# Every TensorE instruction of a hybrid decoder step kept in the order in which the program emits it

## The chip, the cores and the metric

The kernel runs on one core of one Trainium2 chip, in one launch. The time is device microseconds of that core. The core's engines take instructions each from a queue of its own, in that queue's order, and wait for each other on semaphores: TensorE (PE; its weight loads are shown apart as PEld), VectorE (DVE), ScalarE (ACT), GpSimd (POOL) and SyncE (SP), which here issues all the DMA transfers.

## The reference, cut to what matters

One layer of a hybrid decoder, for a prompt of 2048 tokens and for 8 sequences of 8 sample tokens, in float32. Three head groups share one RMSNorm, one input projection and one output projection:

```python
u = rmsnorm(h, norm_w)
proj = u @ w_in                      # 1024 -> z, xbc, dt, gq, gk, gv, gg, glr, sq, sk, sv, sg
y_ssd = ...   # causal conv, silu, chunked state-space scan, gated group norm
y_gla = ...   # decayed linear attention in chunks of 64, per-head norm, silu gate
y_swa = ...   # RMS norm of q and k, window-128 attention with bias and sinks, silu gate
mix = concat([y_ssd, y_gla, y_swa]) @ w_out
h = h + mix
h = h + sigmoid(h @ w_pg) * (p @ w_pe)
```

It returns the two outputs and the new states and caches.

## The kernel before, in words

The tokens are cut into 8 blocks of 256 (17 tiles of 128, the last of them the 64 sample tokens, which ride with block 1). A product in float32 accuracy is made of three products of rounded parts (high by high, high by low, low by high), so a projection unit is 24 matmuls into one PSUM tile: `dense_F` (features on the partitions, 256 columns, or 320 in block 1), `dense_T` (tokens on the partitions, 280 or 512 columns). `mm` (L204) and `tr` (L207) are the helpers that issue nearly every matmul and transpose, the latter also on TensorE.

The kernel goes through the blocks in stages. In G it normalizes and transposes x (`prep_chain`: x tile in X7 or X8, transposes `pt`, then `uh` and `ul` by ACT L326 and DVE L327), projects q, k (`pq`, `pk_`), v and gates (`pT`) and runs the linear attention (`gla_a`: `ptl`, `py`; `gla_b`: `pk`, `pa`, `pu`, `po`, `pn`, for the sample tokens also `pos` and `pU`). In W it projects q, k, v of the window attention (`pT`, 512 columns, `u_qkv`), norms them (ACT L688, DVE L690, POOL L691 and L693, DVE L696 and L698), transposes them (`pq`, `swa_turn`), splits them (ACT L729, DVE L730), makes logits `pl`, the softmax (DVE L768, ACT L743), its transposes `ptp` and the output `po`; between them stand the gate units `pg`. S is the convolution and scan (`pfx`, `pfz`, `pbt`, `pcb`, `pxt`, `pys`, `pst`), O the output projection and the last stage the per-layer gate, both by a Strassen-like scheme of seven products (class `Square`, `product`, 12 matmuls of 512 columns each: `pX`, `pY`, `pZ`, `pV`).

Two things set the order of the work. The first is the kernel's own planner, class `Order`: it emits large dense units one after another (each with a cost in us, such as 2.62 for 24 matmuls of 256 columns) and, in between, steps of chains (generators such as `gla_a` or `swa_tile`) as soon as they are due on its running sum of costs. How long a chain's next step is held back is a number in the table `LAT`:

```python
LAT = {
    "x_s": 0.0, "x_t": 2.2, "u": 2.6, "T": 0.3, "glT": 0.0, "A": 10.2, "As": 10.9, "kT": 3.0, ...
    "sqg": 3.3, "ve": 0.8, "qk": 0.5, "kF": 1.4, "qF": 1.7, "sm": 10.8, ...
```

`"qk"` is the time from the end of a `u_qkv` unit to the step that transposes its tile, `"glT"` that from `ptl` to `py`. The second is the scheduler of the tile framework: it is given the instructions as emitted, and for each engine makes a queue by its own estimate of when each is ready, so that a matmul emitted later may stand ahead of one emitted earlier. That queue is then fixed; the chip does not reorder it. Pools (`psM` three PSUM buffers, `psF` and `psT` two each, `psU` one) make an instruction wait until the buffer it takes is free; the transposes `pt` of blocks 1 to 7 and `pq` of W use `psU`.

Of the kernel before, what the change touches and what calls it, by code (L numbers as in the profile page):

```python
# [149 lines left out]
def hybrid_step(ctx: ExitStack, tc: tile.TileContext, I, C, O):  # L150
    nc = tc.nc
    od = Order()
    PE, V, A, G, SP = nc.tensor, nc.vector, nc.scalar, nc.gpsimd, nc.sync
# [47 lines left out]
        SP.dma_start(out=t, in_=src)  # L201
        return t

    def mm(out, lhsT, rhs, start=True, stop=True):  # L204
        PE.matmul(out, lhsT=lhsT, rhs=rhs, start=start, stop=stop)  # L205

    def tr(out, in_, idn):  # L207
        PE.transpose(out, in_, idn)  # L208


    uh_d = [tc.dram_tile([128, 8, ncols(b)], F32, name=f"uhd{b}") for b in range(NB)]
# [54 lines left out]
    def dense(ps, pairs):  # L266
        n = len(pairs)
        for i, (lh, ll, rh, rl) in enumerate(pairs):
            mm(ps, lh, rh, i == 0, False)
            mm(ps, lh, rl, False, False)  # L270
            mm(ps, ll, rh, False, i == n - 1)
# [36 lines left out]
    def prep_chain():  # L308
        for b in range(NB):
            if b >= 2:  # L310
                yield 0, 0, ("U", b - 2)
            n = ncols(b)
            uh = up.tile([128, 8, n], F32R, tag="uh", name="uh")
            ul = up.tile([128, 8, n], F32R, tag="ul", name="ul")
            for i, (tt, c0, rows) in enumerate(tiles_of(b)):
                if i == 2:
                    load_x(b, i)
                xt = loaded.pop((b, i))
                for q in range(2):
                    yield 0.45, LAT["x_s"] if i == 2 and q == 0 else LAT["x_t"]  # L320
                    pt = mps([128, 4, 128], "pt") if b == 0 else psU.tile([128, 4, 128], F32, tag="u", name="pt")
                    for j in range(4):
                        k = 4 * q + j
                        tr(pt[:, j, :rows], xt[:rows, 128 * k:128 * k + 128], ident[:rows, :rows])
                    o = uh[:, 4 * q:4 * q + 4, c0:c0 + rows]
                    A.activation(out=o, in_=pt[:, :, :rows], func=AF.Copy)  # L326
                    V.tensor_tensor(out=ul[:, 4 * q:4 * q + 4, c0:c0 + rows], in0=pt[:, :, :rows],  # L327
                                    in1=o.bitcast(F32), op=ALU.subtract)
                if b == 0 and i == 0:
                    od.mark("u0", LAT["u"])  # L330
                    us["G", 0] = uh, ul
            us["G", b] = uh, ul
            od.mark(("u", "G", b), LAT["u"])
            SP.dma_start(out=uh_d[b], in_=uh.bitcast(F32))
            SP.dma_start(out=ul_d[b], in_=ul.bitcast(F32))
            for i in range(2):
                if b + 1 < NB:
                    load_x(b + 1, i)
# [137 lines left out]
    def gla_a(b):  # L476
# [5 lines left out]
        for (tt, c0, rows), g in zip(tl, gl):  # L482
            tr(ptl[:, c0:c0 + rows], g[:rows, 0:16], ident[:rows, :rows])
# [38 lines left out]
    def gla_b(b):  # L522
# [6 lines left out]
        for i, (tt, c0, rows) in enumerate(tl):  # L529
            tr(pk[:rows, i, :], kd[:, c0:c0 + rows], ident)  # L530
# [843 lines left out]
    def rows(i):  # L1374
        return 64 if i == NT else 128
# [117 lines left out]
    class Square:  # L1493
# [36 lines left out]
        def product(self, g, n):  # L1530
            R = rows(self.groups[g][0])
            p, akey, bkey = self.prods(g)[n]
            first = p in ("P1", "P6", "P7", "P5") or (self.sample(g) and p == "P3")
            if first:
                self.ps[g, BANK[p]] = self.bank(g, BANK[p])
            ps, a, b = self.ps[g, BANK[p]], self.op[g, akey], ws[self.w, bkey]
            for k in range(4):
                for i, (x, y) in enumerate(((0, 0), (0, 4), (1, 0))):
                    PE.matmul(ps[:R], lhsT=a[:, x, k, :R], rhs=b[:, y + k], start=first and k + i == 0, stop=k == 3 and i == 2,  # L1539
                              skip_group_check=True)  # L1540
            if p == "P6":

                self.u2 = (dk if self.w == "g" else ck).tile([128, 512], F32, tag="u2", name="u2")
                A.activation(out=self.u2[:R], in_=self.ps[g, "X"][:R], func=AF.Copy)
                V.tensor_tensor(out=self.u2[:R], in0=self.u2[:R], in1=ps[:R], op=ALU.subtract if self.sample(g) else ALU.add)
# [329 lines left out]
```

## Time and profile before

| | |
|---|---|
| median of 3 runs | 1224.53 us (1223.22 to 1225.87) |
| the profiled execution: its own time | 1223.86 us |
| its span, first to last instruction | 1222.0 us |
| PE busy | 1168.4 us, 96% |
| PEld busy | 983.9 us, 81% |
| DVE, ACT, POOL busy | 59%, 40%, 36% |
| mean granted TensorE clock | 0.987 |

The span lies 1.9 us below the time of the same execution. A matmul is shown from its start to a modelled end, and the next one starts before that end; the time that a run of matmuls takes is read from one start to the next. "Busy" is the union of these intervals, so the span less PE's busy time, 53.6 us, is the time in which no matmul was in flight. In a timeline row, the text in brackets at the end is the idle time of the engine before it and what ended that. Names are those of the program's tiles without their numbers, so a box that holds many tiles has one name: `X_G` is the x tile (and small vectors) in stage G, `Y_G`, `w_G`, `X_W` other boxes.

### The profile page before, as it was taken

Reading aid. Unit: us, or ns where it says so; the run is one execution under the profiler, and the core shown is the slowest. Engines: PE = TensorE matmul, PEld = TensorE weight load, DVE = VectorE, ACT = ScalarE, POOL = GpSimd, SP = SyncE. Lnnn points to the kernel's source line nnn. Section 1 sums busy time; section 2 is a strip of 40 time slices with the busy share of each in tenths; the row PEclk is TensorE's granted clock in tenths of the full one; section 3 lists DMA queues with packets and bytes.
Section 4 is the critical chain, followed back from the end, with each engine's and each line's share of the span. In section 5 each row is a group of like instructions: output and inputs, shape, how many; then the busy total and the mean of one; then the engine's idle time right before and its main releaser. Section 6 shows DMA issues by size and latency. Waiting matters only on the chain. (4 is left out here: it accounts for less than half of the span.)

```text
span 1222.0 us, 20943 instructions
## 1 busy us (share of the span) xinstructions
PE 1168.4 (96%) x8010; PEld 983.9 (81%) x8010; DVE 720.3 (59%) x1476; ACT 484.4 (40%) x994; POOL 441.8 (36%) x505
## 2 busy tenths in 40 slices
PE   7899999998999999899999999899899999999997
PEld 7787887687888889798799898777778877788886
DVE  4766565744544356478767668877666683444552
ACT  4443434551444445444345435563122352233331
POOL 4222224224521112626534433445445322233431
PEclk8899999999999999899999999999999999999999
DMA  8745465276642237503413333567676432222221
GB/s 249 225 178 194 160 240 165 71 222 178 199 138 100 99 131 229 197 26 129 154 60 121 129 139 97 172 210 238 230 263 212 144 112 87 88 78 78 95 78 52
DMA packets 119036, 182.33 MB, mean 149 GB/s; under 512 B 35573, under 2 KB 88293, under 8 KB 112792
## 3 DMA queue, kind: packets, MB, share of 16 engines
q1 hardware_dynamic: 118936, 180.99, 45.0%
q8 instruction: 63, 1.03, 0.4%
q14 instruction: 37, 0.30, 0.1%
HBM read 125.59 MB, written 55.37 MB: 148 GB/s over the span
## 5 line engine op out<-in xcount | busy, mean ns | idle before, releaser
L205 PE MATMUL pfx<-uh,w 128*128 128x256 f32 (+1 forms) x768 | 151.5, 292 | 3.7 <-ACT Y_S L1094 3.0
L205 PEld LDWEIGHTS pfx<-uh,w 128*128 128x128 f32 x768 | 122.3, 191 | 8.4 <-ACT Y_S L1094 3.7
L205 PE MATMUL pfx<-ul,w 128*128 128x256 f32 (+1 forms) x384 | 110.3, 287 | 0.0
L205 PE MATMUL pfz<-uh,w 128*128 128x256 f32 (+1 forms) x512 | 102.8, 293 | 3.9 <-DVE Y_S L1121 2.5
L205 PE MATMUL pg<-uh,w 128*128 128x256 f32 (+1 forms) x512 | 102.8, 293 | 1.6 <-DVE Y_W L891 1.6
L1690 POOL TENSOR_TENSOR X_C<-ul_D,X_C 128x512 f32<-128x512 f32 (+1 forms) x33 | 43.0, 1303 | 135.7 <-DVE ul_D L1689 111.9
L205 PEld LDWEIGHTS pfz<-uh,w 128*128 128x128 f32 x512 | 82.3, 191 | 7.0 <-DVE Y_S L1121 3.3
L205 PE MATMUL pT<-w,uh 128*128 128x512 f32 (+1 forms) x272 | 87.9, 400 | 0.0
L205 PEld LDWEIGHTS pg<-uh,w 128*128 128x128 f32 x512 | 82.7, 192 | 4.4 <-DVE Y_W L891 1.8
L205 PE MATMUL pg<-ul,w 128*128 128x256 f32 (+1 forms) x256 | 74.6, 292 | 0.0
L205 PEld LDWEIGHTS pfx<-ul,w 128*128 128x128 f32 x384 | 73.2, 191 | 1.5 <-issue 1.3
L205 PE MATMUL pfz<-ul,w 128*128 128x256 f32 (+1 forms) x256 | 74.0, 289 | 0.0
L205 PE MATMUL pT<-Y_G,uh 128*128 128x280 f32 (+1 forms) x272 | 63.5, 317 | 2.7 <-ACT uh L326 2.5
L229 DVE TENSOR_TENSOR w<-raw,w 128x1024 fp32r<-128x1024 f32 x32 | 44.4, 1401 | 29.4 <-ACT w L227 29.4
L227 ACT ACTIVATE w<-raw 128x1024 fp32r<-128x1024 f32 x40 | 41.6, 1056 | 47.2 <-DMA raw<-in_w_in_dram 20.9
L205 PEld LDWEIGHTS pT<-w,uh 128*128 128x128 f32 (+1 forms) x272 | 48.8, 185 | 12.1 <-issue 1.8
L1689 DVE SCALAR_TENSOR_TENSOR ul_D<-ul_D,peC 128x512 f32<-128x512 f32 (+1 forms) x34 | 23.3, 685 | 53.7 <-PE peC L205 48.1
L1539 PE MATMUL pZo<-w,X_C 128*128 128x512 f32 x192 | 48.3, 403 | 6.2 <-DVE X_C L1595 6.2
L205 PE MATMUL pT<-w,ul 128*128 128x512 f32 (+1 forms) x136 | 53.9, 397 | 0.0
L205 PE MATMUL peC<-Y_P,uh_C 128*128 128x512 f32 (+1 forms) x204 | 52.8, 393 | 0.8 <-DVE ul_D L1689 0.8
L205 PEld LDWEIGHTS pT<-Y_G,uh 128*128 128x128 f32 (+1 forms) x272 | 46.2, 197 | 7.5 <-ACT uh L326 3.6
L205 PEld LDWEIGHTS pg<-ul,w 128*128 128x128 f32 x256 | 49.3, 193 | 0.9 <-issue 0.4
(442 smaller groups left out, 2983.2 us busy)
## 6 DMA issues: line engine op xcount, KB each, us to landing
uh<-uhd SPq DMA_DIRECT2D x14, 1024.0 KB
ul<-uld SPq DMA_DIRECT2D x14, 1024.0 KB
raw<-in_w_in_dram SPq DMA_DIRECT2D x17, 512.0 KB
X_G<-in_x_prompt_dram SPq DMA_DIRECT2D x16, 512.0 KB
Y_S<-afd SPq DMA_DIRECT2D x16, 512.0 KB
X_C<-in_x_prompt_dram SPq DMA_DIRECT2D x16, 512.0 KB
ul_C<-mixd SPq DMA_DIRECT2D x16, 512.0 KB
out_y_prompt_dram<-X_C SPq DMA_DIRECT2D x16, 512.0 KB
```

Of the source, the lines that this page charges most:

```text
L205: PE.matmul(out, lhsT=lhsT, rhs=rhs, start=start, stop=stop)
L227: A.activation(out=hi[:, k0:k1], in_=rw, func=AF.Copy, scale=scale)
L229: eng.tensor_tensor(out=lo[:, k0:k1], in0=rw, in1=hi[:, k0:k1].bitcast(F32), op=ALU.subtract)
L1539: PE.matmul(ps[:R], lhsT=a[:, x, k, :R], rhs=b[:, y + k], start=first and k + i == 0, stop=k == 3 and i == 2, skip_group_check=True)
L1689: V.scalar_tensor_tensor(out=th, in0=th, scalar=1.0, in1=pe[:R], op0=ALU.add, op1=ALU.mult)
L1690: eng.tensor_tensor(out=h[:R, cs], in0=th, in1=h[:R, cs], op=ALU.add)
```

## The change

`mm` and `tr` hand each instruction to `tc.keep_in_program_order`, and the products of class `Square` go through `mm` as well, so all matmuls and transposes are covered. The queue of TensorE is then the order of emission, that is the planner's. Other engines' instructions are still placed by the scheduler.

```diff
-    def mm(out, lhsT, rhs, start=True, stop=True):
-        PE.matmul(out, lhsT=lhsT, rhs=rhs, start=start, stop=stop)
+    def mm(out, lhsT, rhs, start=True, stop=True, **kw):
+        tc.keep_in_program_order(PE.matmul(out, lhsT=lhsT, rhs=rhs, start=start, stop=stop, **kw))
 
     def tr(out, in_, idn):
-        PE.transpose(out, in_, idn)
+        tc.keep_in_program_order(PE.transpose(out, in_, idn))
@@
-                    PE.matmul(ps[:R], lhsT=a[:, x, k, :R], rhs=b[:, y + k], start=first and k + i == 0, stop=k == 3 and i == 2,
-                              skip_group_check=True)
+                    mm(ps[:R], a[:, x, k, :R], b[:, y + k], first and k + i == 0, k == 3 and i == 2, skip_group_check=True)
```

The number of instructions on TensorE stays the same. Counted over both queues, the runs of matmuls that follow each other into one PSUM tile go from 1274 to 987.

At the start, TensorE's queue before (`pt_257` and `pt_292` transpose the second x tile, in X8, `pT_264` projects the first tile, `pT_320` the second):

```order
L208 MATMUL pt_243<-ident_127,X7_G_139 128x128 x4
L208 MATMUL pt_250<-ident_127,X7_G_139 128x128 x4
L205 MATMUL pT_264<-Y0_G_147,uh_241 128x280 x2
...
L205 MATMUL pT_264<-Y0_G_147,uh_241 128x280
L208 MATMUL pt_257<-ident_127,X8_G_156 128x128 x4
L208 MATMUL pt_292<-ident_127,X8_G_156 128x128 x4
L205 MATMUL pT_320<-Y0_G_147,uh_241 128x280 x2
L205 MATMUL pq_355<-uh_241,w256_171 128x256
L205 MATMUL pk__388<-uh_241,w256_171 128x256
```

The same stretch after the change (`pt_313` and `pt_348` transpose the third x tile, which is loaded into X7 when the first has been used):

```order
L208 MATMUL pt_250<-ident_127,X7_G_139 128x128 x4
L208 MATMUL pt_257<-ident_127,X8_G_156 128x128 x4
L205 MATMUL pT_264<-Y0_G_147,uh_241 128x280 x2
...
L205 MATMUL pT_264<-Y0_G_147,ul_242 128x280
L208 MATMUL pt_292<-ident_127,X8_G_156 128x128 x4
L208 MATMUL pt_313<-ident_127,X7_G_139 128x128 x4
L205 MATMUL pT_320<-Y0_G_147,uh_241 128x280 x2
```

The transposes of x tiles now stand ahead of projections that need no new tile: `pt_257` ahead of all of `pT_264`, `pt_313` ahead of all of `pT_320`. Before, `pt_313` stood behind `pT_320`, `pq_355` and nearly all of `pk__388`. Further on the queue has `pt_348`, `pq_355`, `pt_381`, `pk__388`, `pt_432`, `pt_444`, `ptl_451`, `py_455`, `pt_473`, `pt_494`, `pq_501`, `pt_527`, `pk__534`, `pt_560`, and only then the `pT`, `pa`, `pu` and `po` of blocks 0 and 1.

In stage G, TensorE's queue before, from `ptl_1704` (the low-rank gate input transposed; DVE L485 copies it to SBUF) to `py_1708`, which reads that copy:

```order
L205 MATMUL pu_1683<-Y2_G_128,X9_G_198 32x64 x16
L208 MATMUL ptl_1704<-ident_127,Y2_G_128 16x128 x2
L205 MATMUL pq_1772<-ul_1439,w256_171 128x256
...
L205 MATMUL pT_1876<-Y0_G_147,uh_1438 128x280
L205 MATMUL py_1708<-w_G_193,Y2_G_128 128x256
```

And after:

```order
L205 MATMUL pu_1683<-Y2_G_128,X9_G_198 32x64 x16
L208 MATMUL ptl_1704<-ident_127,Y2_G_128 16x128 x2
L205 MATMUL py_1708<-w_G_193,Y2_G_128 128x256
L208 MATMUL pt_1726<-ident_127,X8_G_156 128x128 x4
L205 MATMUL po_1733<-X9_G_198,Y2_G_128 64x128 x8
```

The matmuls that stood between the two are gone from there. It is so at six of the eight blocks.

In stage W, TensorE's queue before, at the transposes `pq_3416` of tile 6 (whose projection is `pT_3377`; `pT_3440` is that of tile 7):

```order
L205 MATMUL pT_3377<-w512_414,ul_3051 128x512
L205 MATMUL pT_3440<-w512_414,uh_3050 128x512
...
L205 MATMUL po_3410<-X8_W_2518,X6_W_2207 64x256 x2
L205 MATMUL po_3410<-X8_W_2518,Y1_W_2146 64x256 x2
L208 MATMUL ptp_3426<-ident_127,Y1_W_2146 128x128 x4
L208 MATMUL ptp_3432<-ident_127,Y1_W_2146 128x128 x4
...
L208 MATMUL pq_3416<-ident_127,X6_W_2207 128x128 x3
L205 MATMUL pT_3440<-w512_414,uh_3050 128x512
```

And after:

```order
L205 MATMUL pT_3377<-w512_414,ul_3051 128x512
L205 MATMUL po_3410<-X8_W_2518,X6_W_2207 64x256 x2
L205 MATMUL po_3410<-X8_W_2518,Y1_W_2146 64x256 x2
L208 MATMUL pq_3416<-ident_127,X6_W_2207 128x128 x3
L208 MATMUL ptp_3426<-ident_127,Y1_W_2146 128x128 x4
L208 MATMUL ptp_3432<-ident_127,Y1_W_2146 128x128 x4
L205 MATMUL pT_3440<-w512_414,uh_3050 128x512
```

Only `po_3410` is left between the end of a tile's projection and its transposes. For the odd tiles (`pT_3440`, `pq_3510`) it is twelve `pl` and four `po`, and behind `pq_3510` one unit `pg_3548` and then the `pl` that need its result. In each block from 3 to 7 it is the same; block 2 has no `po` at these places, and the 18 `pos` of the sample tokens at the first.

## Rows read from the trace of the kernel before

**Rows 1.** Busy time by stretch: window, its length, busy us per engine, clock, DMA share.
```profile
0.00:62.35 62.35, 52.98 (x342) 45.70 (x343) 34.92 (x58) 27.59 (x50) 21.21 (x38) 0.86 0.77 240
62.35:190.00 127.65, 127.15 (x1147) 106.08 (x1146) 76.82 (x160) 55.36 (x118) 36.41 (x59) 1.00 0.51 182
190.00:460.00 270.00, 264.14 (x1872) 218.79 (x1871) 136.31 (x463) 110.22 (x328) 76.94 (x103) 0.99 0.46 148
460.00:1222.00 762.00, 724.17 (x4655) 613.32 (x4653) 472.28 (x796) 291.21 (x500) 307.26 (x306) 0.99 0.42 137
```
**Rows 2.** Timeline of the start: start us, duration us, engine, line, operation, tiles.
```profile
12.15 0.60 PE L205 MATMUL pT<-Y_G,uh 128*128 128x280 f32 x1 [1.82 <-ACT uh L326]
14.64 1.28 DVE L304 SCALAR_TENSOR_TENSOR X_G<-X_G 128x1024 f32<-128x1024 f32 x1 [0.57 <-POOL X_G L303]
...
26.63 1.28 DVE L304 SCALAR_TENSOR_TENSOR X_G<-X_G 128x1024 f32<-128x1024 f32 x1 [0.44 <-POOL X_G L303]
...
40.14 0.29 PE L205 MATMUL pT<-Y_G,ul 128*128 128x280 f32 x1
...
40.52 0.29 PE L205 MATMUL pT<-Y_G,ul 128*128 128x280 f32 x1
...
50.44 1.28 DVE L304 SCALAR_TENSOR_TENSOR X_G<-X_G 128x1024 f32<-128x1024 f32 x1 [0.77 <-POOL X_G L303]
...
62.35 0.60 PE L208 MATMUL pt<-ident,X_G 128*128 128x128 f32 x4
```
**Rows 3.** Timeline: the first `py`, behind its `ptl`.
```profile
31.77 0.69 PE L205 MATMUL py<-w_G,Y_G 16*128 16x256 f32 x2 [2.13 <-DVE w_G L485]
```
**Rows 4.** Lines L485, L326 and L327: duration ns min/median/max, first and last start.
```profile
L485 DVE COPY w_G<-ptl x8: 402/408/479, 31.3 to 201.2; 16x256 f32<-16x256 f32 x7, 16x320 f32<-16x320 f32 x1
L326 ACT ACTIVATE uh<-pt x34: 363/597/600, 11.5 to 175.4; 128x512 fp32r<-128x512 f32 x32, 128x256 fp32r<-128x256 f32 x2
L327 DVE TENSOR_TENSOR ul<-pt,uh x34: 418/684/694, 12.8 to 176.5; 128x512 fp32r<-128x512 f32 x32, 128x256 fp32r<-128x256 f32 x2
```
**Rows 5.** Timeline of one W tile, from its projection's end (PE, ACT, POOL, DVE).
```profile
407.38 0.65 PE L205 MATMUL po<-X_W,Y_W 128*64 128x256 f32 x4
...
408.39 1.09 PE L208 MATMUL ptp<-ident,Y_W 128*128 128x128 f32 x8
...
408.97 0.73 POOL L906 TENSOR_TENSOR X_W<-X_W,Y_W 128x256 f32<-128x256 f32 x1
...
409.66 1.35 POOL L693 TENSOR_TENSOR X_W<-X_W,mhalf 128x6 f32<-128x6 f32 x1
...
411.45 0.28 DVE L698 TENSOR_TENSOR X_W<-pT,X_W 128x128 f32<-128x128 f32 x1
```
**Rows 6.** Timeline of another W tile, from its transposes to its logits.
```profile
330.01 0.44 PE L208 MATMUL pq<-ident,X_W 128*128 128x128 f32 x2
...
334.43 0.45 ACT L729 ACTIVATE X_W<-pq,X_W 128x256 fp32r<-128x256 f32 x1
...
337.96 0.38 PE L205 MATMUL pl<-X_W 64*128 64x256 f32 x2
...
338.86 0.86 PE L205 MATMUL pl<-X_W 64*128 64x256 f32 x10
```
**Rows 7.** Chain of waits: a whole product and one cut by another unit.
```profile
1003.45 0.93 PE pXg L1539 x4
...
1005.75 1.82 PE pXg L1539 x8
...
1012.58 2.74 PE pXg L1539 x12
```
**Rows 8.** Timeline: the longest wait in W.
```profile
304.92 0.38 PE L205 MATMUL pl<-X_W 64*128 64x256 f32 x2 [3.15 <-ACT X_W L729]
```
**Rows 9.** Busy time of the 3.4 us behind that wait, columns as in rows 1.
```profile
305.80:309.20 3.40, 3.40 (x20) 3.18 (x21) 3.26 (x10) 1.80 (x9) 1.93 (x3) 0.50 0.50 143
```

## The prediction

> **What bounds the kernel now.** I read the busy table first: TensorE is busy 1168.4 of 1222.0 us, the next engine 59%. The kernel is bound by TensorE, and the change adds no work to it, so the question is what happens to the 53.6 us in which no matmul is in flight, and whether new idle time appears. Second came the busy time by stretch [rows 1]: idle is 9.4 us in the start, 0.5 in stage G, 5.9 in W and 37.8 in the rest (S, O and the last stage). G and W are thus nearly closed already, and it is there that the order of TensorE changes most, because chains and dense units are woven most closely there. Third I read the timelines at places where the new order puts a consumer right behind its producer, to get how long the chain between the two takes on the other engines [rows 2 to 6]. The scheduler's order had filled these chains with later dense matmuls; in a pinned queue TensorE stands still for what the emitted cover does not fill. The planner holds a chain step back by its table only, and two entries are far below what the trace shows: 0.0 from `ptl` to `py`, where the row shows 2.13 us of waiting [rows 3], and 0.5 from a window projection to its transposes, where the chain took 4.3 us [rows 5].
>
> **The change part by part.** The sum is made against the profiled execution: 1223.86 us, 1.9 above its span and 0.7 below the median of the runs.
>
> *Start, +12 (8 to 15).* X8 holds the second x tile only from 14.64 + 1.28 = 15.92 us [rows 2]. Before, TensorE began the first `pT` at 12.15; after, `pt_257`, which reads X8, stands ahead of it. The third tile is ready at 26.63 + 1.28 = 27.91, and `pt_313` now stands ahead of the whole of `pT_320`, so that `pT_320`, `pq_355` and `pk__388` no longer fill that wait. The fifth is ready at 50.44 + 1.28 = 51.72 [rows 2]; SP issues the same loads in the same order, so I take these times over. From there the queue has `pt_494` (about 0.5), its rounding in ACT and DVE (0.60 + 0.68 [rows 4], 1.4 with hand-offs), `pq_501`, `pt_527`, `pk__534` and then `pt_560`. A `pT` unit is 24 matmuls, three in 40.52 - 40.14 = 0.38 us [rows 2], so 3.05; with 320 columns in place of 280 it is 3.5. That makes 51.72 + 0.5 + 1.4 + 3.5 + 0.4 + 3.5 = 61.0, with a hand-off some 61.5. Before, this `pt` started at 62.35 [rows 2], 0.85 later, but by then it had also done three `pT` units (9.2) and block 0's small matmuls (about 5.5), of which 1.9 in sum are overlaps and a transpose that the new order has done too. 9.2 + 5.5 - 1.9 - 0.85 = 12.0.
>
> *Stage G, +16 (9 to 22).* With 0.5 us idle before, nothing can be won. At six of the eight blocks `py` stands right behind `ptl`, at five of them newly so. The copy L485 takes 0.41 [rows 4]; with the drain ahead of it the wait is at least 0.65, at most the 2.13 of the first block, where the clock was low; I take 1.0, so 5.0. The transposes of the next x tile share one PSUM buffer, which is free when L326 and L327 have read it (0.60 + 0.68 [rows 4]): four pairs with nothing or little between them, 1.4, 1.4, 0.9 and 0.7, make 4.4. The sample tokens' chain `pn`, `pt`, `pn`, `pU` has no matmul of others between its steps: nine steps on ACT and DVE of the size of these lines (0.4 to 0.7), about 6.0. One more `pn` takes 0.8. Sum 16.
>
> *Stage W, +38 (18 to 60).* From the end of a tile's projection (407.38) to the end of its last norm step (411.45 + 0.28 = 411.73) the chain took 4.35 [rows 5]. In it POOL's L906 (0.73) stood ahead of L693 (1.35); without that it is 3.6. For an even tile the new order leaves only `po` between, 408.39 - 407.38 = 1.0: a wait of 2.6 to 3.35, taken as 3.2. For an odd tile there are twelve `pl` besides (0.38 + 0.86 [rows 6]), 2.25 in all: 1.35 to 2.1, taken as 1.3, since POOL's extra step is the even tile's. Behind the odd `pq` stands one `pg` unit, 24 x 0.127 x 256/280 = 2.8, and then `pl`, which needs the split. In the trace the split took from 330.45 to 337.96 = 7.5, 4.0 of it until L729 came up at 334.43 behind the softmax on ACT [rows 6]. Without that queue the wait is 7.5 - 4.0 - 2.8 = 0.7, with all of it 4.7. In the new order the softmax has the 1.0 of `po` and the 1.3 of wait as a lead, which leaves 2.4; I take 2.0. Together 6.5 per pair of tiles, and six pairs (tiles 4 to 15): 39. In early W two `pq` pairs on one PSUM buffer (2.0 each by L729 and its like) and a `po` (0.8) add 5. W's own idle time of 5.9 went to other waits of the same chains, and these I count as replaced: 39 + 5 - 5.9 = 38.
>
> *S, O, the last stage: 0 (-10 to +10).* They have 37.8 us of idle, the most to win, but the new order keeps one or two dense units between producer and consumer there as the old one did. A product cut in two by another unit costs nothing: 0.93 + 1.82 = 2.75 against 2.74 whole [rows 7].
>
> *Fewer seams, -6 (-29 to 0).* There are 287 fewer changes between accumulating runs. The row just named prices one at 0.01 us; small transposes between projections lose somewhat more. I take 0.02, and 0.1 as the far end.
>
> *Clock, +4 (0 to 14).* After a wait of 3.15 us [rows 8] the granted clock was 0.50, 1.2 GHz, for 3.4 us at full work [rows 9], which costs 1.7. The even tiles' waits of about 3.2 are of that length; I let some of the six, and one or two of stage G, do it. The Trainium skill ("TensorE: Matmul & The Clock Gate", section "HAM oscillation — how this bites in real kernels") says that idle gaps between bursts of matmuls throttle the clock anew each time. By that rule all six would pay, 10 in place of 4; the rows here show one such wait in W, and it agrees.
>
> 12 + 16 + 38 + 0 - 6 + 4 = +64. The span becomes 1286, the time with 1.9 around it **1288 us**.
>
> **The rivals.**
> *The waits are smaller* (1240 to 1265). The chains run at their short values, since engines that have nothing else queued answer sooner, and waits that follow each other overlap: start 8, G 9, W 18, clock 0, seams -6 make +29, time 1253. For it: the split without its queue is 0.7. Against it: W's norm chain is all serial, and 3.6 is its floor.
>
> *The waits are larger* (above 1310). The split keeps the softmax ahead of it (4.7 rather than 2.0, six times, +16), each wait of 3 us and more drops the clock (+10), and start and G are at their upper ends (+9): +35 on the forecast, 1323. For it: the softmax did stand ahead in the trace [rows 6].
>
> *Whole batches win* (faster). TensorE runs units unbroken. The Trainium skill ("Perfetto Trace Analysis", section "Matmul Optimizations") says that matmuls should execute back to back in batches. As a mechanism of this kernel: 287 seams at 0.1 are 29 us, while chain consumers no longer cut into units; it decides where the cover in the new order is longer than the chain, as it may be in S and O. If start, G and W then cost nothing, the time is 1195. Against it: cutting cost 0.01 [rows 7], and in W only 1.0 us of work covers a chain of 3.6.
>
> *The change does nothing*, because the planner's order and the scheduler's come to the same: 1224. The rows of the order speak against it at each of the three places shown.
>
> **How the numbers follow.** The forecast (1265 to 1310) gets 0.55, smaller waits 0.22 (nearly all above 1240), larger waits 0.17, faster 0.04, nothing 0.02. The range holds 8 in 10: it leaves out about 0.04 at the top, the faster and idle cases and the lower half of the smaller waits: 1250 to 1324. About 0.2% is what this kernel's measurement can tell from no change; faster 0.04, same 0.02, slower 0.94.
>
> **What would show it.** Right: idle in W grows from 5.9 to 40 to 50, with `pq` waiting for DVE's L698 or L696 at each even tile for about 3 us and `pl` for L729 or L730 behind odd ones; `py` waits for L485 at about 1 us; the first `pT` starts behind 15.92 and the transposes of tile 5 still near 51.7; PE busy, less the stretches at the low clock, stays near 1168. Wrong: if `pq` does not wait in W, the planner's cover is longer than I read it; if S, O and the last stage change by over 10 us in either direction, their zero fails; if PE busy falls by 15 us or more, the seams were dear.

## The result and the profile after

The changed kernel takes 1409.68 us (median of 4 runs, 1406.74 to 1416.56) against 1225.2 us: 1.1499 times as long, 95% interval 1.1462 to 1.1536. The direction was forecast; the size, 184 us, is almost three times the 64 us of the forecast and far above the range. The profiled execution took 1416.56 us, with a span of 1414.8; TensorE is busy 1218.2 us of it and idle 196.6, and the mean granted clock is 0.919 where it was 0.987. The span grew by 192.8 us: 143.0 more idle time, and 49.8 more busy time for the same matmuls.

Busy time by stretch, after; the stretches are about start and G, W, S, and O with the last stage (columns as in [rows 1]):

```profile
0.00:240.00 240.00, 199.06 (x1591) 166.06 (x1592) 121.21 (x238) 89.07 (x179) 62.15 (x109) 0.89 0.50 174
240.00:590.00 350.00, 285.49 (x1887) 241.68 (x1887) 139.79 (x476) 119.31 (x345) 73.19 (x104) 0.90 0.38 119
590.00:985.00 395.00, 328.08 (x2702) 298.72 (x2703) 229.05 (x431) 147.94 (x249) 142.59 (x179) 0.89 0.31 100
985.00:1414.80 429.80, 405.55 (x1833) 326.20 (x1831) 235.01 (x333) 135.34 (x223) 154.56 (x114) 0.98 0.41 138
```

The reader is to see that idle time is 41, 65 and 67 us in the first three stretches and that the clock is near 0.9 in all of them; the fourth has 24 us of idle time, part of it late work of S. Stages overlap at their edges, so I also counted by matmul: each one's time is from its start to the next one's, and idle time goes to the matmul that ends it.

| stage of the matmul | time before | after | idle before | after |
|---|---|---|---|---|
| start and G | 198.6 | 239.3 | 9.9 | 40.9 |
| W with its gates | 263.5 | 332.5 | 5.9 | 59.8 |
| S | 338.9 | 417.5 | 18.7 | 75.7 |
| O and the last | 413.0 | 417.4 | 13.9 | 14.9 |

What TensorE waited for, the longest sums (us in total, times, longest us):

```profile
PE pq L208 <- DVE X_W L696: 36.9, 12, 7.9
PE pxt L208 <- DVE Y_S L1056: 27.6, 4, 11.1
PE pxt L208 <- DVE X_S L1056: 15.4, 3, 6.3
PE pt L208 <- DVE X_G L304: 13.0, 3, 6.3
PE pq L208 <- DVE X_W L730: 11.1, 2, 8.2
```

`pq` behind the norm chain of W was forecast. `pxt` behind L1056, the silu that ends the convolution of S, was not: 43 us, more than W's norm chain.

The start, timeline after: the second x tile's `pt` and the third's wait for the scaled tile, within 0.4 us of the times worked out from [rows 2], and `py` waits for L485 at 0.50 us where the clock is full (2.13 in [rows 3]).

```profile
16.28 0.45 PE L208 MATMUL pt<-ident,X_G 128*128 128x128 f32 x1 [6.26 <-DVE X_G L304]
27.68 0.48 PE L208 MATMUL pt<-ident,X_G 128*128 128x128 f32 x1 [5.25 <-DVE X_G L304]
...
212.41 0.48 PE L205 MATMUL py<-w_G,Y_G 16*128 16x256 f32 x1 [0.50 <-DVE w_G L485]
```

One pair of W tiles, timeline after, to be read against [rows 5, 6]:

```profile
463.44 1.08 PE L205 MATMUL po<-X_W 128*64 128x256 f32 x8
467.45 0.87 PE L208 MATMUL pq<-ident,X_W 128*128 128x128 f32 x3 [2.93 <-DVE X_W L696]
468.11 1.92 PE L208 MATMUL ptp<-ident,Y_W 128*128 128x128 f32 x8
...
479.37 0.72 PE L208 MATMUL pq<-ident,X_W 128*128 128x128 f32 x3 [1.34 <-DVE X_W L696]
483.74 0.39 PE L205 MATMUL pl<-X_W 64*128 64x256 f32 x2 [0.79 <-ACT X_W L729]
484.64 0.86 PE L205 MATMUL pl<-X_W 64*128 64x256 f32 x10 [0.52 <-DVE X_W L730]
```

The even tile waits 2.93 us, the odd one 1.34, `pl` 0.79 + 0.52. The same three come back to a hundredth in three other pairs. The `ptp` behind the first wait take 1.92 us where they took 1.09 [rows 5]. Two windows tell why: the stretch up to that `pq`, and the 3.4 us behind it.

```profile
463.00:467.45 4.45, 1.52 (x11) 0.57 (x10) 0.90 (x3) 0.88 (x2) 2.27 (x3) 1.00 0.43 173
467.80:471.20 3.40, 3.40 (x14) 3.07 (x14) 0.67 (x2) 2.21 (x5) 0.00 (x0) 0.50 0.00 0
```

After 2.93 us without a matmul the granted clock is 0.50 (1.2 GHz) while TensorE works at full load, as in [rows 8, 9]. It is so behind, or from within, all five waits of 2.93 us.

S, timeline after, from the last convolution unit of a block to its `pxt` (PE, ACT, DVE; L1094 and L1051 are the convolution, L1055 and L1056 its silu, L1313 to L1316 the group norm of the block before):

```profile
904.13 0.28 PE L205 MATMUL pfx<-uh,w 128*128 128x256 f32 x1
904.25 0.27 PE L208 MATMUL pbt<-ident,X_S 128*128 128x128 f32 x1
904.45 0.49 PE L205 MATMUL pcb<-X_S 64*128 64x128 f32 x4
904.73 0.56 ACT L1094 ACTIVATE X_S<-pfx,Y_S 128x256 f32<-128x256 f32 x1
904.87 1.13 PE L205 MATMUL pn<-Y_S 128*128 128x512 f32 x2
905.48 1.28 ACT L1313 ACT_TABLE_LOAD   x1
905.84 0.38 PE L208 MATMUL pxt<-ident,X_S 128*128 128x128 f32 x2
906.77 0.69 ACT L1313 ACTIVATE Y_S<-pn,epst 128x512 f32<-128x512 f32 x1
907.01 0.47 DVE L1051 SCALAR_TENSOR_TENSOR X_S<-X_S,Y_S 128x256 f32<-128x256 f32 x1
907.48 1.28 ACT L1314 ACT_TABLE_LOAD   x1
909.43 1.27 DVE L1316 SCALAR_TENSOR_TENSOR Y_S<-Y_S 128x256 f32<-128x256 f32 x3 [1.95 <-ACT Y_S L1314]
910.63 0.48 DVE L1051 SCALAR_TENSOR_TENSOR X_S<-X_S,Y_S 128x256 f32<-128x256 f32 x1
911.14 0.63 ACT L1055 ACTIVATE X_S<-X_S 128x512 f32<-128x512 f32 x1 [1.74 <-DVE X_S L1051]
911.80 0.69 DVE L1056 SCALAR_TENSOR_TENSOR X_S<-X_S 128x512 f32<-128x512 f32 x1 [0.30 <-ACT X_S L1055]
912.54 0.69 PE L208 MATMUL pxt<-ident,X_S 128*128 128x128 f32 x2 [6.33 <-DVE X_S L1056]
```

Between the last `pfx` and the `pxt` that needs its silu TensorE has about 2 us of small work, and the chain takes 8.3 us from 904.25 to 912.54. DVE's last L1051 stands in its queue behind L1316, which waits 1.95 us for ACT, which loads two function tables of 1.28 us; the L1051 before it ended at 907.48, the last one starts at 910.63, 3.15 us later. Before the change the same place looked like this (timeline before, PE, another block):

```profile
702.47 0.28 PE L205 MATMUL pfx<-uh,w 128*128 128x256 f32 x1
702.59 0.28 PE L205 MATMUL pfz<-uh,w 128*128 128x256 f32 x1
...
710.11 0.38 PE L208 MATMUL pxt<-ident,Y_S 128*128 128x128 f32 x2
```

Between the two rows stand 60 matmuls of `pfz`, and `pxt` does not wait: there, too, 7.6 us lie between the last `pfx` and this `pxt`, but they are full of work. It was so, with 36 to 72 matmuls of `pfz`, in seven of the eight blocks.

### The profile page after: what moved, and what is told of

It reads as the page before. It is cut to its first block, busy times and chain, and to the rows that moved or that the text cites. A ratio compares the mean times of both kernels' runs of the same rounds, so it can differ in the third digit from the quotient of the medians.

```text
span 1414.8 us, 20980 instructions
## 1 busy us (share of the span) xinstructions
PE 1218.2 (86%) x8010; PEld 1032.7 (73%) x8010; DVE 725.1 (51%) x1476; ACT 491.7 (35%) x994; POOL 432.5 (31%) x505
## 5 line engine op out<-in xcount | busy, mean ns | idle before, releaser
L205 PEld LDWEIGHTS pfx<-uh,w 128*128 128x128 f32 x768 | 127.1, 198 | 9.3 <-ACT X_S L1153 3.0
L205 PE MATMUL pfz<-uh,w 128*128 128x256 f32 (+1 forms) x512 | 112.5, 313 | 0.0
L205 PE MATMUL pg<-uh,w 128*128 128x256 f32 (+1 forms) x512 | 108.3, 305 | 0.0
L205 PEld LDWEIGHTS pfz<-uh,w 128*128 128x128 f32 x512 | 92.5, 215 | 1.5 <-DVE X_S L1224 0.9
L205 PEld LDWEIGHTS pg<-uh,w 128*128 128x128 f32 x512 | 89.0, 207 | 1.2 <-issue 0.4
L205 PE MATMUL pfz<-ul,w 128*128 128x256 f32 (+1 forms) x256 | 79.0, 308 | 0.0
L205 PEld LDWEIGHTS pT<-w,uh 128*128 128x128 f32 (+1 forms) x272 | 53.2, 201 | 12.5 <-issue 1.3
L205 PE MATMUL pT<-Y_G,uh 128*128 128x280 f32 (+1 forms) x272 | 57.0, 306 | 0.0
L205 PEld LDWEIGHTS pfz<-ul,w 128*128 128x128 f32 x256 | 55.1, 215 | 0.0
L208 PE MATMUL pq<-ident,X_W 128*128 128x128 f32 (+1 forms) x51 | 12.7, 357 | 48.0 <-DVE X_W L696 36.9
```

The source lines that it names most:

```text
L205: tc.keep_in_program_order(PE.matmul(out, lhsT=lhsT, rhs=rhs, start=start, stop=stop, **kw))
L208: tc.keep_in_program_order(PE.transpose(out, in_, idn))
```

## The experiments

**Does each stage lose by its own order?** Four kernels pin the matmuls and transposes of some stages only. The edit, with the functions of that stage in `PIN`:

```diff
+    PIN = {"u_x", "u_z", "ssd_front", "ssd_x", "ssd_chunk", "ssd_sample", "ssd", "s_norm"}
+    def kept(ins):
+        f, by = sys._getframe(2), set()
+        while f:
+            by.add(f.f_code.co_name)
+            f = f.f_back
+        if by & PIN:
+            tc.keep_in_program_order(ins)
```

> Only the matmuls and transposes that stage G issues (x transposes, q, k, v and gate projections, linear attention) are pinned behind the one emitted before them; all others are placed by the scheduler, as in the kernel before. Theory A (each stage loses by its own order): stage G's matmuls took 198.6 us of TensorE's time before and 239.3 after, so about +41: 1266 us, with the first matmul of the third x tile waiting about 5 us for DVE L304 and the sample chain's pn 5 us for ACT L602. Theory B (the loss comes from the queues of ACT and DVE getting out of step over the whole program): a part alone costs much less than its share, under +20: below 1245.

> Only the matmuls and transposes that stage W issues (window attention and its gate units) are pinned. Theory A: W took 160.5 + 103.0 us before and 226.5 + 106.0 after, so about +69: 1294 us, with pq waits of 2.9 us for DVE L696 at even tiles and about as many stretches at half clock as in W after. Theory B: matmuls of S, which are free to move, fill the waits, or the chains run at their short values: under +30, below 1255.

> Only the matmuls and transposes that stage S issues (convolution, scan, group norm) are pinned. Theory A: S took 338.9 us before and 417.5 after, so about +79: 1303 us, with pxt waiting about 6 us for DVE L1056 in most blocks. Theory B: S is late in the changed kernel only because W hands it late and disordered data; alone it costs under +30, below 1255.

> Only the matmuls and transposes of the output projection, the last gate and their embedding are pinned; 60 of the 287 changes between accumulating runs go. Theory A: the parts measured so far make 37 + 81 + 64.5 = 182.5 of 184.5 us, so this one is 0 to +4: 1224 to 1228 us. Rival (longer unbroken runs of matmuls are a gain where nothing waits): 60 seams at 0.08 us, a figure worked out from both traces, make -5: 1219 us.

| pinned | ratio to before, 95% | excess |
|---|---|---|
| start and G | 1.0299 (1.0250 to 1.0347) | 0.030 |
| W | 1.0660 (1.0547 to 1.0774) | 0.066 |
| S | 1.0526 (1.0491 to 1.0560) | 0.053 |
| O and the last | 1.0074 (1.0047 to 1.0102) | 0.007 |
| sum of the four | | 0.156 |
| all | 1.1499 (1.1462 to 1.1536) | 0.150 |

In us over the kernel before, the parts cost 37, 81, 65 and 10, where 41, 69, 79 and 0 to 4 were expected. They make up the whole: the four intervals taken together leave about 0.013 either way on their sum, an estimate, and it is 0.006 above the whole. Theory A holds: each stage loses in its own order and no stage needs the disorder of another. The waits of the whole are there in the part; what TensorE waited for when only S is pinned:

```profile
PE pxt L219 <- DVE Y_S L1067: 27.5, 4, 11.0
PE pxt L219 <- DVE X_S L1067: 15.6, 3, 6.3
```

(L1067 is the silu's L1056, eleven lines further down.) O and the last stage came out slower by 0.7%, above the expected 0 to 0.3%, and not faster as their 60 fewer seams would have it.

**W: cover between a projection and its transposes.** `"qk": 0.5` becomes `"qk": 4.6`; all stays pinned.

> The changed kernel with LAT qk 4.6 in place of 0.5, so that the planner puts one more projection or gate unit between a window projection and its transposes. Theory A (uncovered chain): the waits of 2.93 (six) and 1.35 (five) us before pq vanish, 24 us, and with them five to seven stretches at half clock of 3.4 us, 10 us: 1375 us; the waits of 1.3 us before pl stay. Rival: the wait only moves behind pq, to pl, since the split and the softmax are what W waits for in the end: 1400 to 1410 with pl waits of 3 us and more.

1361.85 us, ratio 1.1102 (1.1053 to 1.1151): 48 us less, more than the 35 expected. Idle time at W's matmuls falls from 59.8 to 17.6 us, more than the regular waits: the irregular ones before `pq` go too. Two tiles, timeline of this kernel:

```profile
404.29 0.49 PE L208 MATMUL pq<-ident,X_W 128*128 128x128 f32 x3
408.46 0.98 PE L205 MATMUL pl<-X_W 64*128 64x256 f32 x12
410.38 0.55 PE L208 MATMUL pq<-ident,X_W 128*128 128x128 f32 x3
414.24 1.25 PE L205 MATMUL pl<-X_W 64*128 64x256 f32 x12 [0.46 <-ACT X_W L729]
```

`pq` waits no more (48.0 us in all before this edit). A small part of the wait moved: `pl` waits 11.2 us in all where it waited 5.2, and `pbt` of S 10.6 where it waited 4.7. One number of the planner's table was the cause of W's regular waits.

**The clock: does it fall for the idle time?** Transposes whose result nobody uses are put where TensorE waited:

```diff
+        for _ in range(0 if tt < 4 or rows < 128 else 12 if tt % 2 else 26):
+            tr(pq[:, 0], ident, ident)
...
+            for _ in range({0: 24, 2: 64, 6: 18, 8: 50, 10: 52, 12: 52, 14: 92}.get(tt, 0) if m == 2 else 0):
+                tr(px[:, 3], ident, ident)
```

> The changed kernel with idle time of TensorE filled by transposes whose result nobody uses: 26 (even tiles) and 12 (odd tiles) ahead of pq in W from tile 4 on, and 18 to 92 ahead of the third pxt transpose in the blocks where it waited, 508 in all, sized a little under each wait. Theory C (the clock falls for the idle time ahead of it): the stretches at half clock in W from 380 us on and at the pxt waits vanish, some 87 us of stretches with about 60 us busy, 30 us gained less a few us of overhang: 1380 to 1390 us although TensorE does more. Rival (the half clock has other causes, such as the change of load or the engine's own work): no gain, 1410 to 1430.

The edit adds 580 transposes (the expectation counts 508). With them the kernel takes 1394.22 us, ratio 1.1394 (1.1338 to 1.1449), which is below the changed kernel's interval: TensorE does more and the time falls by 13 to 15 us. The same place as above, windows of this kernel over the filled wait and the 3.4 us behind it:

```profile
458.80:462.00 3.20, 3.20 (x31) 2.83 (x27) 0.71 (x3) 0.38 (x1) 2.28 (x3) 1.00 0.37 146
462.00:465.40 3.40, 3.40 (x21) 2.93 (x21) 1.17 (x4) 2.10 (x5) 0.00 (x0) 1.00 0.00 0
```

The clock stays at 1.00 (2.4 GHz). Of eight stretches at half clock in W from 380 us on, four are left; the busy time at half clock in the whole kernel goes from 167 to 114 us. The gain is short of the 20 to 30 us expected: some fillings overhang, one of the four stretches is behind a wait that was not filled, and the other three have no wait of over 1 us in the 8 us ahead of them. What made the clock fall there stays open. The Trainium skill ("TensorE: Matmul & The Clock Gate", section "HAM oscillation — how this bites in real kernels") says that idle gaps between bursts throttle the clock each time; the five waits of 2.93 us and this run agree, but a wait of 2.88 us (for `pn` at 974.13 in the changed kernel) has no half clock behind it.

**S: cover behind the convolution.** `"x": 1.8` becomes `"x": 6.5`.

> The changed kernel with LAT x 6.5 in place of 1.8, so that the planner holds the transposes pxt back by about two more projection units after the convolution's last feature unit. Theory A (too little cover on TensorE behind the convolution): most of the 43 us that pxt waits for DVE L1056 go, and the stretches at half clock behind them (about 15 us): 1360 us. Rival (S is bound by DVE and ACT, which are busier there than elsewhere): the waits come back at pys, pcb or pfx, and the time stays above 1395.

1392.75 us, ratio 1.1382 (1.1334 to 1.1429): 17 us less where 50 were expected. `pxt` still waits 18.1 us. The order tells where: the planner had dense units to put in between in blocks 0, 3, 5 and 7 (three `pfz`, 8.9 us), but none in blocks 4 and 6, since `z_units` let a `pfz` go only when the norm of the block before is done; there `pxt` follows its producer at once. In block 6:

```profile
883.51 0.28 PE L205 MATMUL pfx<-uh,w 128*128 128x256 f32 x1
884.84 0.41 PE L208 MATMUL pxt<-ident,X_S 128*128 128x128 f32 x2 [1.05 <-DVE X_S L1056]
891.23 0.69 PE L208 MATMUL pxt<-ident,X_S 128*128 128x128 f32 x2 [5.98 <-DVE X_S L1056]
```

So theory A had the right cause and the wrong lever. The next kernel makes the norm due earlier as well: `"qk": 4.6`, `"x": 6.5`, `"y2": 3.0`.

> The changed kernel with LAT qk 4.6, x 6.5 and y2 3.0. Counted from the orders, the matmuls that stand between the last convolution unit of a block and its pxt (the cover) are in the changed kernel 3.0, 0.4, 5.8, 3.0, 0.4, 0.8, 0.8 and 3.4 us for blocks 0 to 7, and the waits were 2.96, 7.70, 0, 2.45, 6.10, 6.33, 6.33 and 11.09: cover and wait make 5.5 to 8 us. Here the cover is 3.4 us in block 4, 3.3 in block 6 and 5.9 to 8.9 in all others. Theory A (wait = chain of 6 to 7 us less cover): pxt waits about 3 us in blocks 4 and 6 and under 1 us elsewhere, against 43 us in all; with 48 us for qk the time is 1315 to 1330 us. Rival: the waits move to pn, pys or pfz, since DVE and ACT cannot do S faster: above 1345.

1326.21 us, ratio 1.0788 (1.0738 to 1.0839), within the expected 1315 to 1330; of the 184 us, some 85 are back. Block 4, with 3.4 us of cover:

```profile
750.54 0.56 PE L208 MATMUL pxt<-ident,X_S 128*128 128x128 f32 x2 [3.97 <-DVE X_S L1056]
```

Block 6 waits 3.97 us too, block 1 (cover 5.9) 0.9, blocks 0, 3 and 5 nothing. From the last `pfx` of a block to the `pxt` that needs its silu the changed kernel takes 5.8 to 9.1 us at the waits (15.2 in block 7), the run named x65 7.7 and 7.9 in blocks 4 and 6; that is the chain. Here blocks 4 and 6 take 10.9 and 10.5, because a `pn` in between waits 2.4 and 2.0 us itself, for POOL's L1307: part of the rival's move came about, within the time that was expected. One wait of 6.3 us in block 7 was not expected, and I did not find its cause.

**S: is it the queue?** First the group norm's two table loads are taken out (Ln becomes Identity, Exp becomes Copy; this part of the computation is left out).

> The changed kernel with the group norm of S left without its logarithm and exponential (Ln becomes Identity, Exp becomes Copy; this part of the computation is left out), so that ACT loads no function tables there. The queues of ACT and DVE hold this norm between the last convolution step and the silu that pxt waits for, and the two table loads take 1.28 us each. Theory Q (head of the queue): four of the pxt waits of 6.1 to 7.7 us fall by 2.6 us each or more, 10 us, with the clock some 15: 1395 us. Theory A alone (short cover): the norm is beside the point, the waits stay at 6 us, time within 5 us of 1410.

The wait at the place shown falls from 6.33 to 4.32 us, three others by 2.0 to 2.3, the sum of `pxt` waits from 43.0 to 31.9. The time, 1401.74 us, ratio 1.1455 (1.1411 to 1.1499), is not clear of the changed kernel's. So the norm's loads are 2 us of the chain. The Trainium skill ("ScalarE: Activation LUTs", section "What ACT_TABLE_LOAD costs") gives 1283 ns for a load and 1380 ns more for a drain; the rows above show the load of L1313 (1.28), and its activation starting at 906.77, 1.29 after the load did, so the drain does not show.

Then VectorE's and ScalarE's instructions of S are kept in emission order too, so that the convolution stands ahead of the norm:

```diff
+            def call(*a, **k):
+                ins, f, by = getattr(self.eng, name)(*a, **k), sys._getframe(1), set()
...
+                if by & {"u_x", "u_z", "ssd_front", "ssd_x", "ssd_chunk", "ssd_sample", "ssd", "s_norm"}:
+                    tc.keep_in_program_order(ins)
...
+    V, A = Kept(nc.vector), Kept(nc.scalar)
```

> The changed kernel, and in stage S also every VectorE and ScalarE instruction kept behind the one emitted before it on its engine, so that the last convolution steps and the silu stand ahead of the group norm of the block before, as emitted. Theory Q (the pxt waits are long because the norm, waiting for ACT, stands at the head of DVE's queue ahead of the convolution): the four waits of 6.1 to 7.7 us fall to the bare chain of about 2 to 2.5 us, S loses some 16 us of idle and four to six stretches at half clock less: 1385 us. Theory A alone (too little work on TensorE, the queues are beside the point): waits within 1 us of 6, time 1405 to 1415. Rival: the emission order of DVE and ACT stalls elsewhere in S: slower than 1415.

> The kernel of the run named da_s with LAT qk 4.6 and x 6.5 as well. If the three repairs work on different waits they add: 1410 less 48 (qk), less 17 (x), less what da_s gains, about 1320 to 1330 us. If x and da_s take away the same wait, as theory Q says, x adds little to it: 1335 to 1345 us.

1442.88 us, ratio 1.1768 (1.1684 to 1.1853), 33 us slower than the changed kernel; with the two table entries 1392.67 (1.1359, 1.1276 to 1.1441), nowhere near 1320 to 1345. So the rival of the first expectation holds. The waits of 6.3 fell to 4.5, not to 2 to 2.5, and one of 24.5 us came up (most line numbers are those of the wrapper; the last three rows are from the timeline, DVE's the silu that was L1056, ACT's the norm's L1313):

```profile
PE pbt L226 <- DVE X_S L162: 24.5, 1, 24.5
...
919.82 0.69 DVE L162 SCALAR_TENSOR_TENSOR X_S<-X_S 128x512 f32<-128x512 f32 x1 [0.76 <-ACT X_S L162]
921.27 0.69 ACT L162 ACTIVATE Y_S<-pn,epst 128x512 f32<-128x512 f32 x1
922.01 0.90 PE L226 MATMUL pxt<-ident,X_S 128*128 128x128 f32 x3 [4.50 <-ACT Y_S L162]
```

With the norm out of the way, the silu is done at 920.51, 3.0 us into this wait; the last 1.5 us TensorE waits, by the profile, for ACT, whose norm now comes late. So theory Q holds for about half of such a wait (3.15 us at the place shown in the changed kernel, 2 of them the table loads), and its lever loses more elsewhere: idle time at S's matmuls goes from 75.7 to 105.0 us. The other half is the convolution's own work, six L1051 of 0.48 us and the steps around them, in either order.

**All table entries at once**, stage G's as well:

> The changed kernel with the planner's table set for the chains as the trace shows them: qk 4.6, x 6.5, glT 0.9, pa 0.9, sqg 6.5, ve 1.7, x_t 3.4. Theory A: the gains of the single entries add (48 for qk, 50 for x, some 15 for stage G): 1295 to 1310 us. Rival: moving one wait uncovers the next, since the dense units that cover one chain are taken from another: 1330 us or more.

1361.23 us, ratio 1.1124 (1.1082 to 1.1166). W and S gained nearly as in the runs named qk46 and x65, but idle time at G's matmuls rose from 40.9 to 50.7 us: `pt` waits 14.4 in place of 23.0, and `pT`, which did not wait, 8.3. The rival holds for G. No kernel tried here reaches the time before, and no edit took the waits of start and G away; that they are the cause there rests on the trace and on the kernel that pins G alone.

## Why the prediction was wrong

| term | forecast | shown |
|---|---|---|
| start and stage G, idle | +28 | +31.0 |
| W, idle | +38 | +53.9 |
| S, O and the last, idle | 0 | S +57.0, O and the last +1.0 |
| seams, and all else at full clock | -6 | -13 to -30 |
| clock | +4 | +62 to +79 |
| sum | +64 | +192.8 |

The idle rows are from the table by matmul. The last two share the 49.8 us of busy time, and the traces do not split it sharply. The busy time at half clock is 26.2 us before and 167.2 after; if half of it is lost, that is 13.1 and 83.6, a difference of 70.5, and what remains is 49.8 - 70.5 = -20.7. A second way takes, for each kind of matmul, the mean time from one start to the next at full clock, less idle time, times its number: 1155.8 us before and 1143.1 after, -12.7. With only those matmuls that no idle time follows it is 1149.6 and 1120.0, -29.6. The table gives these two ends.

- *Start and G* were right in size and in most places. The x tiles come at 16.28 and 27.68; the one forecast for 51.7, on which the start's sum was built, did not hold TensorE up, since DVE had scaled it at 49.0, so that part of the +12 is luck. The pairs on one PSUM buffer wait 1.41 against 1.4, `py` 0.50 to 0.72 against 1.0, the sample chain about 9.5 against 6.0.
- *W's regular waits* were right: 2.93, 1.34 and 1.31 against 3.2, 1.3 and 2.0. What was missing are four irregular ones (8.2, 7.9, 6.6 and 4.1 us). The one of 7.9 us has a row: ACT's queue held L688, the first step of that tile's norm, behind L989, which belongs to the prelude of S and waited 10.25 us for a transfer.

```profile
354.71 0.21 ACT L989 ACTIVATE Y_S<-Y_S 128x8 f32<-128x8 f32 x1 [10.25 <-DMA Y_S<-in_a_log_dram]
354.86 0.49 ACT L688 ACTIVATE X_W<-pT 128x384 f32<-128x384 f32 x1
```

- *S at nothing* is the first step that failed. The prediction said that the new order keeps one or two dense units between producer and consumer there. At four of eight blocks it keeps only small matmuls (1.4 to 2.1 us), and the chain of the convolution, which the prediction did not measure, takes some 6 to 9 us, so that even one unit (3.0 us, blocks 0 and 3) leaves 2.5 to 3.0 us of wait. More cover took most of them away, 43.0 us of `pxt` waits falling to 15.1 in the run named lat_y3; that is shown.
- *The clock at 4* is the second, and the larger one: the mechanism was right and its size was not. The prediction gave it to some of six waits. In fact every wait of 2.9 us and more in this trace has half clock behind it, and so have some of 2.3 to 2.8 (not all: one of 2.88 and one of 2.68 have none); there are over thirty stretches, four of them behind no wait of over 1.4 us, of 3.4 to 20.5 us. Each long wait so costs more than its own length. That idle time is the cause is shown for the waits that were filled; that all of the 62 to 79 us come from it was not tried.
- *The seams* stay open. Matmuls at full clock gained 13 to 30 us, against 6, and small ones show it: `pl` takes 74 ns from start to start after and 97 before, `po` of 256 columns 110 and 146 (means over those that no idle time follows). Counted at the changes alone it is less. In the kernel before, a `pl` with another tile's matmul behind it takes 248 ns to the next start, one with its own behind it 72; `po` of 256 columns 310 and 109. Such extra times, summed over all kinds and changes between tile names, make 20.9 us before and 14.2 after, 6.7 less, which is the forecast. No run separates the rest, and pinning O and the last stage alone, with 60 fewer changes, gained nothing. This gain is what the rival of whole batches was about; the waits and the clock cost at least seven times as much (143 + 62 to 79).

The rival "larger waits" named two of the right mechanisms, clock and queue, but priced them at 26 us, for W alone; waits in S were in none of the rivals.

## What to carry to other kernels

When an order is taken from a scheduler and given to a planner, list every place where the planner lets a consumer follow its producer, stage by stage, and measure the chain for each, with what stands ahead of it in the queues of the engines between; a stage with the most idle time before is not safe for that reason. Price each new wait of some 3 us on a matrix engine at its length and then the time at half clock behind it. A planner's delay is only as good as the work that it is free to put in: where dense units wait for something themselves, a longer delay alone brings nothing.

## What the hardware showed that was not expected

Adding 580 useless transposes to the engine that sets the end made the changed kernel faster by about 1%, because they kept its clock at 1.00 over waits that had dropped it to 0.50. And a small matmul takes longer to the next start where another tile's matmul stands behind it: `pl` 248 ns against 72, `po` of 256 columns 310 against 109, at full clock in the kernel before; a product of 512 columns cut in two shows 0.01 us [rows 7].
